# Reciprocal square roots on GpSimd instead of a ten-step VectorE chain

## The chip, the cores and the metric

The kernel runs on one core of one Trainium2 chip. The metric is the device time of one execution in microseconds (us). A profile of one execution shows the core's engines: TensorE (PE; its weight loads are PEld), VectorE (DVE), ScalarE (ACT), GpSimd (POOL), and SyncE (SP), which here issues DMA transfers.

## What is computed

One layer of a hybrid decoder trunk on 1024 tokens of width 1024, in float32: a half feed-forward, a mixer with eight gated-delta heads and sixteen Mamba-2 heads, a second half feed-forward, and a last norm.

```python
def rms_norm(x, w):
    y = x * lax.rsqrt(jnp.mean(x * x, axis=-1, keepdims=True) + EPS)
    return y * w

def l2_normalize(x):
    return x * lax.rsqrt(jnp.sum(x * x, axis=-1, keepdims=True) + EPS)

def reference(x, ...):
    x = x + 0.5 * swiglu(rms_norm(x, ffn1_norm[i]), ffn1_w_gate[i], ffn1_w_up[i], ffn1_w_down[i])
    x = x + hybrid_mixer(rms_norm(x, mix_norm[i]), w_in[i], ...)   # delta heads: l2_normalize of q and k,
                                                                   # rms_norm of each head's output
    x = x + 0.5 * swiglu(rms_norm(x, ffn2_norm[i]), ffn2_w_gate[i], ffn2_w_up[i], ffn2_w_down[i])
    return rms_norm(x, final_norm)
```

Every norm has one reciprocal square root per token (per token and head in the delta heads, per token and group in the Mamba-2 gate norm).

## The kernel before

The tokens lie in eight blocks of 128 (NB = 8), one token per partition, so the reciprocal roots of a block are one column of 128 values. Each big product is made of three passes of TensorE with operands split in a high and a low part (`mm3`, lines 121 to 123; lines 332 to 334 and 552 to 554 are the same three passes in the feed-forwards).

The stages in time: the start (blocks loaded, the first half of the blocks normalised in two pairs by `normalise_pairs`, the second half by `normalise(1, ...)`, transposes on TensorE, splits, first gate and up products); the first feed-forward; at its end `norm_first` (blocks 0 to 3, called while the last products of the down projection run) and `norm_second` (blocks 4 to 7, in two pairs); projections and the Mamba-2 heads (about 700 to 1000 us); the delta heads (about 1000 to 1560 us); the out projection, with `normalise(0, ...)` and `normalise(1, ...)` for the second feed-forward; that feed-forward; and `finish`, block by block, for the last norm.

`rsqrt_into` (line 109) is called at each of these places. It makes a first guess from the bits of the value (line 112) and refines it in three rounds of three VectorE instructions (lines 116 to 118): ten instructions, each reading what the one ahead wrote. The input tile is `ssv` (mean square plus epsilon), the output `rstd`; in the Mamba-2 gate norm they are `sv` and `rg`, in the delta heads `tk` and `rin`, `sso` and `co`. What reads the output differs: at the start lines 207 and 208 (in place, on ScalarE and VectorE), in `normalise` lines 186 and 188, in `norm_second` lines 741 and 742 (output `xn`), in `finish` lines 1456 and 1457 (output `xw`). Scaled blocks then go through TensorE's transposes (`transposed`, line 216, into the PSUM tiles `ps_sc`, two buffers), from which ScalarE and VectorE make the operands (`keepx`, `bh`, `bl`, `hhi`, `hlo`).

The program is written in a tile framework. Its scheduler puts each engine's instructions in an order of its own, from the dependences and its estimates of costs; the hints `tc.issue_after` hold some back. On the chip each engine runs its own list strictly in order and waits at an instruction until its inputs are there. GpSimd's list holds, besides constants and the first small loads, 36 memsets of `pre`, 24 selects of 128x1024 (`md`, `dt`) and some memsets for the heads. `ah` is the high part of a gate or up weight (`wst` when it comes from the staging tile), `as` the gate and up weights' sum, `wd` and `hid` the down projection's operands.

Of the kernel before, what the change touches and what calls it, by code (L numbers as in the profile page):

```python
# [11 lines left out]
F32 = mybir.dt.float32  # L12
F32R = mybir.dt.float32r
I32 = mybir.dt.int32
BF16 = mybir.dt.bfloat16
AF = mybir.ActivationFunctionType
ALU = mybir.AluOpType
# [4 lines left out]
P = 128  # L22
L = 1024
D = 1024
NB = L // P
# [19 lines left out]
def kernel(  # L45
# [7 lines left out]
    V, A, G, T = nc.vector, nc.scalar, nc.gpsimd, nc.tensor  # L53
# [3 lines left out]
    const = ctx.enter_context(tc.tile_pool(name="const", bufs=1))  # L57
# [25 lines left out]
                    pattern=[[1, P]], channel_multiplier=-1)  # L83
    ones = const.tile([P, P], F32, name="ones")
    G.memset(ones, 1.0)
    cols = const.tile([P, 96 + 48 + 12 + 9 + 24], F32, name="cols")
    cw_g = cols[:, 0:96].rearrange("p (t c) -> p t c", t=4)
    cw_s = cols[:, 96:144].rearrange("p (t c) -> p t c", t=4)
# [17 lines left out]
        return last, V.tensor_copy(cols, pc[:, 0:189])  # L106


    def rsqrt_into(pool, y, v, tag):

        n = v.shape[1]
        V.tensor_scalar(out=y.bitcast(I32), in0=v.bitcast(I32), scalar1=-0.5,
                        scalar2=1597463007.0, op0=ALU.mult, op1=ALU.add)
        t = pool.tile([P, n], F32, name="rs_t", tag=tag)
        for _ in range(3):
            V.scalar_tensor_tensor(out=t, in0=y, scalar=-0.5, in1=v, op0=ALU.mult, op1=ALU.mult)
            V.tensor_tensor(out=t, in0=t, in1=y, op=ALU.mult)
            V.scalar_tensor_tensor(out=y, in0=t, scalar=1.5, in1=y, op0=ALU.add, op1=ALU.mult)

    def mm3(o, wh, wl, mh, ml, first, last):  # L120
        T.matmul(o, lhsT=wh, rhs=mh, start=first, stop=False)  # L121
# [39 lines left out]
    def rms_stats(pool, xt, b0, nb, junk):  # L161
        ss = pool.tile([P, nb], F32, name="ss")
        for i in range(nb):
            A.activation(out=junk, in_=xt[b0 + i], func=AF.Square, accum_out=ss[:, i:i + 1])
        v = pool.tile([P, nb], F32, name="ssv")
        V.tensor_scalar(out=v, in0=ss, scalar1=1.0 / D, scalar2=EPS, op0=ALU.mult, op1=ALU.add)
        r = pool.tile([P, nb], F32, name="rstd")
        rsqrt_into(pool, r, v, "rst")
        return r

    def normalise(half, pool, xt, tags=None, jtag=None):
# [20 lines left out]
    def normalise_pairs(pool, xt, jtag):  # L192

        junk = ha.tile([P, 2, D], BF16, name="junk2", tag=jtag)
        sums = [pool.tile([P, 2], F32, name="ss") for _ in range(2)]
        A.activation(out=junk[:, 0], in_=xt[0], func=AF.Square, accum_out=sums[0][:, 0:1])
        V.scalar_tensor_tensor(out=junk[:, 1], in0=xt[1], scalar=1.0, in1=xt[1],
                               op0=ALU.mult, op1=ALU.mult, accum_out=sums[0][:, 1:2])
        for i in range(2):
            sq = A.activation(out=junk[:, 0], in_=xt[2 + i], func=AF.Square, accum_out=sums[1][:, i:i + 1])  # L200
        for i in range(2):
            v = pool.tile([P, 2], F32, name="ssv")
            V.tensor_scalar(out=v, in0=sums[i], scalar1=1.0 / D, scalar2=EPS, op0=ALU.mult, op1=ALU.add)
            r = pool.tile([P, 2], F32, name="rstd")
            rsqrt_into(pool, r, v, "rst")
            with tc.issue_after(sq.ins):
                A.mul(out=xt[2 * i], in_=xt[2 * i], mul=r[:, 0:1])
            last = V.tensor_scalar(out=xt[2 * i + 1], in0=xt[2 * i + 1], scalar1=r[:, 1:2], scalar2=None,
                                   op0=ALU.mult)
        return xt[0:4], last  # L210
# [476 lines left out]
    with ExitStack() as c1:  # L687
        npool = NormPool(ffn_pools(c1))
        H = {}
        with tc.tile_pool(name="x1", bufs=1, side="right", reuse_waits="tile") as xp, \  # L690
                tc.tile_pool(name="keep", bufs=1, side="right", reuse_waits="tile") as kp:
            xt = blocks(xp, "xt")
            for b in range(4):
                nc.sync.dma_start(out=xt[b], in_=x_v[:, b])
            last_t, cols_in = load_cols(npool)
            raws = [a_load(ffn1_w_gate[0], 0), a_load(ffn1_w_up[0], 0)]
            for b in range(4, NB):
                nc.sync.dma_start(out=xt[b], in_=x_v[:, b])
            ops = [{}, {}]
            x0, last = normalise_pairs(npool, xt, "h6")  # L700
            with tc.issue_after(last.ins), tc.issue_after(cols_in.ins):
                a_start(npool, raws, ops, 0)
            r11, r22 = (kp.tile([P, 4, 512], F32, name=f"keepx{i}") for i in range(2))
            with tc.issue_after(last_t.ins):
                b_first(npool, x0, nrm[0], H, r11)
            x1 = normalise(1, npool, xt, jtag="h7")
            a_start(npool, raws, ops, 1)
            last = b_second(npool, x0, x1, nrm[0], H, r11, r22,
                     start_rest(npool, H, ffn1_w_gate[0], ffn1_w_up[0], raws, ops))
        dn = gate_up_phase(0, npool, H, ffn1_w_gate[0], ffn1_w_up[0], ffn1_w_down[0], raws, ops, last)  # L710

        xp = c1.enter_context(tc.tile_pool(name="x1b", bufs=1, side="right", reuse_waits="tile"))
        xt = blocks(xp, "xtb")
        h2 = []

        def norm_first():
            h2.extend(new_ht())
            for b in range(4):
                nc.sync.dma_start(out=x_scr[:, b], in_=xt[b])
            norm_ht(0, normalise(0, npool, xt), nrm[1], *h2)  # L720

        ss = const.tile([P, 8], F32, name="ss2")
        xns = []

        def square(i, dh):
            junk = npool.tile([P, 512], BF16, name="junk", tag="q")
            A.activation(out=junk, in_=xt[4 + i][:, dh * 512:(dh + 1) * 512], func=AF.Square,
                         accum_out=ss[:, 4 * dh + i:4 * dh + i + 1])

        def norm_second(i):  # L730
            square(i, 0)
            nc.sync.dma_start(out=x_scr[:, 4 + i], in_=xt[4 + i])
            if i % 2 == 0:
                return
            v = npool.tile([P, 2], F32, name="ssv")
            V.tensor_tensor(out=v, in0=ss[:, i - 1:i + 1], in1=ss[:, 3 + i:5 + i], op=ALU.add)
            V.tensor_scalar(out=v, in0=v, scalar1=1.0 / D, scalar2=EPS, op0=ALU.mult, op1=ALU.add)
            r = npool.tile([P, 2], F32, name="rstd")
            rsqrt_into(npool, r, v, "rst")
            xn = hbp[0].tile([P, 2, D], F32, name="xn", tag=("b3", "b0")[i // 2])  # L740
            A.mul(out=xn[:, 0], in_=xt[3 + i], mul=r[:, 0:1])
            V.tensor_scalar(out=xn[:, 1], in0=xt[4 + i], scalar1=r[:, 1:2], scalar2=None, op0=ALU.mult)
            xns.extend((xn[:, 0], xn[:, 1]))
            if i == 3:
                h2.append(norm_ht(1, xns, nrm[1], *h2))

        def before_last():
            load_gates_w()
            prefetch()

        with tc.tile_pool(name="dtmp0", bufs=1, reuse_waits="tile") as dtmp:
            down_all(dtmp, xt, x_v, dn, [before_last], norm_first, lambda i: square(i, 1), norm_second)
        hhi, hlo, last_h = h2

    cm = ExitStack()
    gp = cm.enter_context(tc.tile_pool(name="gates", bufs=1, reuse_waits="tile"))
# [53 lines left out]
    with tc.tile_pool(name="gtmp", bufs=1, side="right", reuse_waits="tile") as tp:  # L810
# [48 lines left out]
        for c in (15, 13, 11, 9, 7, 5, 3):  # L859
# [8 lines left out]
                               in1=alog.unsqueeze(1).to_broadcast([P, NB, NG]),  # L868
# [31 lines left out]
    for un in range(4):  # L900
# [138 lines left out]
        if un % 2 == 1:  # L1039
            pc = psum("mx")  # L1040
            for b in range(NB):
                T.matmul(pc[:, 2 * b:2 * b + 2], lhsT=sq[:, b * P:(b + 1) * P], rhs=ones[:, 0:2],
                         start=True, stop=True)
            sv = const.tile([P, NB], F32, name=f"sv{grp}")
            V.tensor_scalar(out=sv, in0=pc[:, 0:2 * NB].rearrange("p (b c) -> p b c", c=2)[:, :, 0],
                            scalar1=1.0 / 512.0, scalar2=EPS, op0=ALU.mult, op1=ALU.add)
            rg = const.tile([P, NB], F32, name=f"rg{grp}")
            rsqrt_into(gp, rg, sv, "rst")
            rstd_g.append(rg)
    cs_.close()  # L1050

# [49 lines left out]
    with ExitStack() as cg:  # L1101
        g1 = cg.enter_context(tc.tile_pool(name="gdn1", bufs=1, reuse_waits="tile"))
        g2 = cg.enter_context(tc.tile_pool(name="gdn2", bufs=2, reuse_waits="tile"))
        for h in range(GH):
# [59 lines left out]
            vr = g2.tile([P, NB, P], F32, name="vr")  # L1164
            ssq = g2.tile([P, NB], F32, name="ssq")
            rin = g2.tile([P, NB], F32, name="rin")
            rsqrt_into(g2, rin, tk, "rst")
            V.tensor_tensor(out=rin, in0=rin, in1=tk, op=ALU.mult)
            for half in range(2):
                pt = psum("mx")  # L1170
# [131 lines left out]
                A.activation(out=jk, in_=vr[:, b], func=AF.Square, accum_out=sso[:, b:b + 1])  # L1302
            V.scalar_tensor_tensor(out=sso, in0=sso, scalar=1.0 / P, in1=cq, op0=ALU.mult, op1=ALU.add)
            co = g2.tile([P, NB], F32, name="co")
            rsqrt_into(g2, co, sso, "rsto")
            V.tensor_tensor(out=vr, in0=vr, in1=co.unsqueeze(2).to_broadcast([P, NB, P]), op=ALU.mult)
            nc.sync.dma_start(out=mix_scr[h // 2][:, :, hl * P:(hl + 1) * P], in_=vr)

# [139 lines left out]
    def finish(i):  # L1448
# [2 lines left out]
        V.scalar_tensor_tensor(out=v, in0=ss[:, i:i + 1], scalar=1.0 / D, in1=ss[:, 4 + i:5 + i],  # L1451
                               op0=ALU.mult, op1=ALU.add)
        r = npool.tile([P, 1], F32, name="rstd")
        rsqrt_into(npool, r, v, "rst")
        o = xw[i // 2][:, i % 2]
        A.mul(out=o[:, 512:], in_=o[:, 512:], mul=r)
        V.tensor_scalar(out=o[:, 0:512], in0=o[:, 0:512], scalar1=r, scalar2=None, op0=ALU.mult)
# [28 lines left out]
```

## Time and profile before

| | |
|---|---|
| time, median of 3 runs | 2310.83 us (2310.03 to 2311.5) |
| span of the profiled execution | 2309.8 us |
| PE busy | 2275.9 us, 99% |
| DVE busy | 1726.7 us, 75%, 3349 instructions |
| ACT busy | 1096.0 us, 47% |
| POOL busy | 53.6 us, 2%, 125 instructions |
| DMA traffic | 281.33 MB, mean 122 GB/s |

Of the profiled execution the span is known, 2309.8 us, and no other time; the median of the runs lies 1.03 us above it. Busy is the time in which an engine had an instruction running. In a row of a timeline the first number is the start in us from the start of the span, the second the duration in us; the brackets at the end give the engine's idle time ahead of it and what ended that.

### The profile page before, as it was taken

The page shows a single profiled execution, that of the slowest core. Times are in us where ns is not written, and L with a number is a line of the kernel's source. Part 1 is how long each engine was busy: PE and PEld are TensorE (multiplying, and loading weights), DVE is VectorE, ACT ScalarE, POOL GpSimd, SP SyncE. Part 2 cuts the span into 40 slices and gives each one's busy share as a digit, 9 for nine tenths or more (in the row PEclk, how much of TensorE's full clock was granted, in tenths as well). Part 3 has the DMA queues.
Part 4 walks back from the last instruction along what each step waited for, and adds up shares of the span by engine and source line. Part 5 has one row for each costly group of instructions (what it writes and reads, how often), then busy time and mean ns, then how long its engine had stood idle before and what let it go on. Part 6 is the DMA issues. An engine that isn't in the chain of part 4 may idle for free.

```text
span 2309.8 us, 31485 instructions
## 1 busy us (share of the span) xinstructions
PE 2275.9 (99%) x11766; PEld 1868.7 (81%) x11766; DVE 1726.7 (75%) x3349; ACT 1096.0 (47%) x1990; POOL 53.6 (2%) x125
## 2 busy tenths in 40 slices
PE   7999999999999999999999999999999999999998
PEld 5788888888878888888888888888878888888886
DVE  7977776767765675668778888778698777766787
ACT  7433333343367785864455556422543333334344
POOL 0000000000000100000000000000000000000000
PEclk9999999999999999999999999999999999999999
DMA  3333332573652322222333222335223333329456
GB/s 111 125 114 103 105 108 98 175 279 129 220 180 78 92 92 74 72 86 74 83 101 82 73 83 61 116 98 192 91 83 116 111 102 105 109 88 349 141 156 214
DMA packets 220957, 281.33 MB, mean 122 GB/s; under 512 B 47008, under 2 KB 153564, under 8 KB 219780
## 3 DMA queue, kind: packets, MB, share of 16 engines
q1 hardware_dynamic: 220548, 279.23, 37.4%
q8 instruction: 92, 1.51, 0.3%
q14 instruction: 61, 0.50, 0.1%
q0 software_dynamic: 256, 0.10, 0.0%
HBM read 211.55 MB, written 67.73 MB: 121 GB/s over the span
## 4 chain that ended last, share of the span: by engine, by line
PE 89%; DVE 5%; ACT 2%; DMA 1%; issue 1%; SPq 0%; POOL 0%; DVEq 0%; ACTq 0%
PE ps_pj L123 11%; PE ps_pj L122 10%; PE ps_pj L121 10%; PE ps_pj L332 6%; PE ps_pj L334 6%; PE ps_pj L333 6%; PE ps_mx L332 3%; PE ps_mx L334 3%; PE ps_mx L333 3%; PE ps_pj L553 2%; PE ps_pj L554 2%; PE ps_pj L552 2%; PE ps_oo L334 2%; PE ps_oo L333 2%; PE ps_oo L332 2%; PE ps_sc L552 1%
## 5 line engine op out<-in xcount | busy, mean ns | idle before, releaser
L123 PE MATMUL ps_pj<-hhi,wlo 128*128 128x512 f32 x832 | 334.3, 402 | 0.0
L121 PE MATMUL ps_pj<-hhi,whi 128*128 128x512 f32 x832 | 332.8, 400 | 0.4 <-ACT gsb L826 0.4
L122 PE MATMUL ps_pj<-hlo,whi 128*128 128x512 f32 x832 | 332.2, 399 | 0.0
L334 PE MATMUL ps_pj<-bh,al 128*128 128x512 f32 x688 | 267.9, 389 | 0.0
L333 PE MATMUL ps_pj<-bl,ah 128*128 128x512 f32 x688 | 267.8, 389 | 0.0
L332 PE MATMUL ps_pj<-bh,ah 128*128 128x512 f32 x688 | 267.5, 390 | 0.0
L121 PEld LDWEIGHTS ps_pj<-hhi,whi 128*128 128x128 f32 x832 | 156.7, 188 | 28.8 <-ACT gsb L826 0.8
L123 PEld LDWEIGHTS ps_pj<-hhi,wlo 128*128 128x128 f32 x832 | 156.7, 188 | 28.5 <-issue 0.7
L122 PEld LDWEIGHTS ps_pj<-hlo,whi 128*128 128x128 f32 x832 | 156.7, 188 | 27.9
L239 ACT CAST ah<-wst 128x512 fp32r<-128x512 f32 x88 | 54.6, 622 | 210.8 <-PE ps_oo L333 125.3
L239 ACT CAST hid<-hraw 128x1024 fp32r<-128x1024 f32 (+1 forms) x84 | 82.3, 981 | 145.5 <-PE ps_oo L554 60.6
L333 PEld LDWEIGHTS ps_pj<-bl,ah 128*128 128x128 f32 x688 | 129.2, 188 | 26.8
L334 PEld LDWEIGHTS ps_pj<-bh,al 128*128 128x128 f32 x688 | 129.1, 188 | 26.6
L332 PEld LDWEIGHTS ps_pj<-bh,ah 128*128 128x128 f32 x688 | 128.9, 188 | 26.6
L315 DVE TENSOR_TENSOR as<-wst 128x512 f32<-128x512 f32 x220 | 145.0, 684 | 2.1 <-DMA wst<-in_ffn_w_up_dram 1.8
L240 DVE TENSOR_TENSOR al<-as,ah 128x512 fp32r<-128x512 f32 x220 | 141.0, 685 | 5.0 <-ACT ah L239 4.5
L332 PE MATMUL ps_mx<-bh,ah 128*128 128x512 f32 x352 | 138.6, 396 | 3.8 <-ACT m L341 1.4
L333 PE MATMUL ps_mx<-bl,ah 128*128 128x512 f32 x352 | 138.2, 393 | 0.4 <-DVE bl L240 0.4
L334 PE MATMUL ps_mx<-bh,al 128*128 128x512 f32 x352 | 137.7, 391 | 0.3 <-DVE al L240 0.3
L239 ACT CAST ah<-as 128x512 fp32r<-128x512 f32 x220 | 125.0, 617 | 20.8 <-DVE as L315 20.8
L240 DVE TENSOR_TENSOR hid<-hraw,hid 128x1024 fp32r<-128x1024 f32 (+1 forms) x84 | 95.0, 1131 | 32.8 <-ACT hid L239 32.5
L341 ACT COPY m<-ps_pj 128x512 f32<-128x512 f32 x88 | 51.5, 588 | 123.1 <-PE ps_pj L334 120.9
(448 smaller groups left out, 5118.9 us busy)
## 6 DMA issues: line engine op xcount, KB each, us to landing
hraw<-hid_scr SPq DMA_DIRECT2D x70, 512.0 KB, 4.4
hid_scr<-hs SPq DMA_DIRECT2D x110, 256.0 KB, 2.3
wst<-in_ffn_w_down_dram SPq DMA_DIRECT2D x50, 512.0 KB, 4.7
wst<-in_ffn_w_gate_dram SPq DMA_DIRECT2D x22, 1024.0 KB, 5.7
wst<-in_ffn_w_up_dram SPq DMA_DIRECT2D x22, 1024.0 KB, 5.4
wst<-in_w_in_dram SPq DMA_DIRECT2D x36, 512.0 KB, 5.2
hid_scr<-sg SPq DMA_DIRECT2D x44, 256.0 KB, 2.0
keep<-in_ffn_w_down_dram SPq DMA_DIRECT2D x20, 512.0 KB, 6.2
```

The lines of the kernel that those rows point to most:

```text
L121: T.matmul(o, lhsT=wh, rhs=mh, start=first, stop=False)
L122: T.matmul(o, lhsT=wh, rhs=ml, start=False, stop=False)
L123: T.matmul(o, lhsT=wl, rhs=mh, start=False, stop=last)
L239: return (A.copy(out=hi, in_=src), V.tensor_tensor(out=lo, in0=src, in1=hi.bitcast(F32), op=ALU.subtract))
L240: V.tensor_tensor(out=lo, in0=src, in1=hi.bitcast(F32), op=ALU.subtract))
L315: V.tensor_tensor(out=t, in0=v[0], in1=v[1], op=v[2])
L332: T.matmul(bank, lhsT=wh[:, k], rhs=bh[:, k], start=a, stop=False, skip_group_check=True)
L333: T.matmul(bank, lhsT=wh[:, k], rhs=bl[:, k], start=False, stop=False, skip_group_check=True)
L334: T.matmul(bank, lhsT=wl[:, k], rhs=bh[:, k], start=False, stop=z, skip_group_check=True)
L341: A.copy(out=t, in_=bank)
L552: T.matmul(bank, lhsT=hh, rhs=wh, start=first and k == 0, stop=False, skip_group_check=True)
L553: T.matmul(bank, lhsT=hh, rhs=wl, start=False, stop=False, skip_group_check=True)
```

## The change

`rsqrt_into` becomes one GpSimd instruction, a power of two tensors: the value and a constant tile `mhalf` of -0.5, filled once at the start by a GpSimd memset. All 31 calls change with it: 310 VectorE instructions go, 31 powers and one memset come, on tiles of 128x1 (4), 128x2 (4), 128x4 (5) and 128x8 (18). The scratch tile `rs_t` goes too.

```diff
+    mhalf = const.tile([P, NB], F32, name="mhalf")
+    G.memset(mhalf, -0.5)
...
-    def rsqrt_into(pool, y, v, tag):
-
-        n = v.shape[1]
-        V.tensor_scalar(out=y.bitcast(I32), in0=v.bitcast(I32), scalar1=-0.5,
-                        scalar2=1597463007.0, op0=ALU.mult, op1=ALU.add)
-        t = pool.tile([P, n], F32, name="rs_t", tag=tag)
-        for _ in range(3):
-            V.scalar_tensor_tensor(out=t, in0=y, scalar=-0.5, in1=v, op0=ALU.mult, op1=ALU.mult)
-            V.tensor_tensor(out=t, in0=t, in1=y, op=ALU.mult)
-            V.scalar_tensor_tensor(out=y, in0=t, scalar=1.5, in1=y, op0=ALU.add, op1=ALU.mult)
+    def rsqrt_into(y, v):
+
+        G.tensor_tensor(out=y, in0=v, in1=mhalf[:, 0:v.shape[1]], op=ALU.pow)
...
-        rsqrt_into(pool, r, v, "rst")
+        rsqrt_into(r, v)
```

The other calls change in the same way. Behind the edit every line number is five lower in the changed kernel (line 207 becomes 202, line 216 becomes 211).

The scheduler orders the engines anew. On ScalarE at the start (`xt` are the blocks, `ah` the high part of the first gate weights, `keepx` the transposed first half), the list before:

```order
L200 ACTIVATE junk_228,ss<-xt 128x1024 x2
L207 ACTIVATE xt<-xt,rstd 128x1024 x2
L239 CAST ah<-wst 128x512
L264 ACTIVATE keepx_281<-ps_sc,cols 128x512
L239 CAST ah<-as 128x512
L239 CAST ah<-wst 128x512
L239 CAST bh_289<-keepx_281 128x512
```

and in the changed kernel:

```order
L195 ACTIVATE junk_230,ss<-xt 128x1024 x2
L234 CAST ah<-wst 128x512
L202 ACTIVATE xt<-xt,rstd 128x1024 x2
L259 ACTIVATE keepx_263<-ps_sc,cols 128x512
L234 CAST ah<-as 128x512
L234 CAST ah<-wst 128x512
L234 CAST ah<-as 128x512
L234 CAST bh_271<-keepx_263 128x512
```

The first cast of the gate weights now stands ahead of the two scalings, and one cast more ahead of `bh`.

On TensorE in `norm_first`, at the first transposes of the scaled blocks (`xtb_3706` to `xtb_3709` before, `xtb_3678` to `xtb_3681` after), the last products of one step of the down projection (four groups of six: three `ps_pj` tiles, then `ps_oo`) stand around them, before:

```order
L554 MATMUL ps_pj_4557<-wd_4943,hid_4944 128x512
L552 MATMUL ps_oo_4558<-wd_4943,hid_4944 128x512
L553 MATMUL ps_oo_4558<-wd_4943,hid_4944 128x512
L216 MATMUL ps_sc_5001<-ident_171,xtb_3706 128x128
L216 MATMUL ps_sc_5008<-ident_171,xtb_3706 128x128
L216 MATMUL ps_sc_5001<-ident_171,xtb_3707 128x128
```

and in the changed kernel:

```order
L549 MATMUL ps_pj_4527<-wd_4915,hid_4916 128x512
L547 MATMUL ps_pj_4528<-wd_4915,hid_4916 128x512
L548 MATMUL ps_pj_4528<-wd_4915,hid_4916 128x512
L211 MATMUL ps_sc_4963<-ident_171,xtb_3678 128x128
L211 MATMUL ps_sc_4963<-ident_171,xtb_3679 128x128
L211 MATMUL ps_sc_4970<-ident_171,xtb_3678 128x128
```

The transposes moved ahead from the second product of the fourth tile (`ps_oo`) to the second product of the second (`ps_pj_4528`): twelve products.

On VectorE at the end (`xt2b` the blocks, `xw` the output; the accumulate into `xt2b` is that of the last block), before:

```order
L116 SCALAR_TENSOR_TENSOR rs_t<-rstd,ssv 128x1
L558 SCALAR_TENSOR_TENSOR xt2b<-ps_oo,xt2b 128x512
L117 TENSOR_TENSOR rs_t<-rs_t,rstd 128x1
L1434 TENSOR_TENSOR xw<-xt2b,wrow 128x512
L118 SCALAR_TENSOR_TENSOR rstd<-rs_t,rstd 128x1
L1451 SCALAR_TENSOR_TENSOR ssv<-ss_18263 128x1
L1457 TENSOR_SCALAR xw<-xw,rstd 128x512
```

and in the changed kernel:

```order
L1446 SCALAR_TENSOR_TENSOR ssv<-ss_18005 128x1
L1452 TENSOR_SCALAR xw<-xw,rstd 128x512
L553 SCALAR_TENSOR_TENSOR xt2b<-ps_oo,xt2b 128x512
L1429 TENSOR_TENSOR xw<-xt2b,wrow 128x512
L1446 SCALAR_TENSOR_TENSOR ssv<-ss_18005 128x1
L1452 TENSOR_SCALAR xw<-xw,rstd 128x512
```

The third block's scaling (line 1457, now 1452), which stood behind the last accumulate, stands ahead of it, and waits there for that block's power on GpSimd.

More of the change, by code (lines that the diff above doesn't have):

```diff
@@ L204, in normalise_pairs @@
             r = pool.tile([P, 2], F32, name="rstd")
-            rsqrt_into(pool, r, v, "rst")
+            rsqrt_into(r, v)
             with tc.issue_after(sq.ins):
@@ L738, in norm_second @@
             r = npool.tile([P, 2], F32, name="rstd")
-            rsqrt_into(npool, r, v, "rst")
+            rsqrt_into(r, v)
             xn = hbp[0].tile([P, 2, D], F32, name="xn", tag=("b3", "b0")[i // 2])
@@ L1047 @@
             rg = const.tile([P, NB], F32, name=f"rg{grp}")
-            rsqrt_into(gp, rg, sv, "rst")
+            rsqrt_into(rg, sv)
             rstd_g.append(rg)
@@ L1166 @@
             rin = g2.tile([P, NB], F32, name="rin")
-            rsqrt_into(g2, rin, tk, "rst")
+            rsqrt_into(rin, tk)
             V.tensor_tensor(out=rin, in0=rin, in1=tk, op=ALU.mult)
@@ L1304 @@
             co = g2.tile([P, NB], F32, name="co")
-            rsqrt_into(g2, co, sso, "rsto")
+            rsqrt_into(co, sso)
             V.tensor_tensor(out=vr, in0=vr, in1=co.unsqueeze(2).to_broadcast([P, NB, P]), op=ALU.mult)
@@ L1453, in finish @@
         r = npool.tile([P, 1], F32, name="rstd")
-        rsqrt_into(npool, r, v, "rst")
+        rsqrt_into(r, v)
         o = xw[i // 2][:, i % 2]
```

## The prediction

> **What bounds the kernel now.** I read the page first: engines, the slices of the span and the head of the chain that ended last.
>
> ```profile
> PE 2275.9 (99%) x11766; PEld 1868.7 (81%) x11766; DVE 1726.7 (75%) x3349; ACT 1096.0 (47%) x1990; POOL 53.6 (2%) x125
> ...
> PE   7999999999999999999999999999999999999998
> ...
> PE 89%; DVE 5%; ACT 2%; DMA 1%; issue 1%; SPq 0%; POOL 0%; DVEq 0%; ACTq 0%
> ```
>
> TensorE is busy in 99% of the span and makes 89% of the chain that set the end. Only the first and the last slice show 7 or 8 tenths. Work taken off VectorE can therefore pay only where TensorE waits, so the next view is TensorE's waits over the whole run, and then a table by stretch (columns: busy time and count of PE, PEld, DVE, ACT, POOL, granted clock, DMA share, GB/s).
>
> ```profile
> PE ps_mx L104 <- DMA colst<-in_gdn_conv_w_dram: 7.4, 1, 7.4
> ...
> PE ps_sc L216 <- ACT xt L207: 2.0, 2, 1.6
> ...
> PE ps_sc L216 <- ACT xtb L186: 1.0, 1, 1.0
> ...
> PE ps_sc L216 <- ACT xt L186: 0.3, 1, 0.3
> ...
> PE ps_sc L216 <- ACT xn L741: 0.3, 1, 0.3
> ...
> 14.50:30.00 15.50, 13.83 (x54) 10.04 (x54) 13.76 (x25) 15.09 (x29) 0.00 (x0) 1.00 0.33 129
> ...
> 1300.00:1500.00 200.00, 198.81 (x1337) 161.99 (x1336) 159.02 (x523) 104.32 (x242) 7.84 (x26) 1.00 0.31 91
> ```
>
> The waits that end in a normalised tile (xt, xtb, xn) are where reciprocal roots stand ahead of TensorE: 2.0 + 1.0 + 0.3 + 0.3 = 3.6 us. The clock column is 1.00, so time lost or won is lost or won in waits. In the middle of the delta-rule heads TensorE is busy 198.81 of 200 us: at most 1.2 us of such a stretch is to be had.
>
> **What goes, and what comes.** One chain, by its first instruction in its four groups, and then all that GpSimd does which could price a power:
>
> ```profile
> L112 DVE TENSOR_SCALAR rstd<-ssv x13: 145/170/171, 7.6 to 2303.7; 128x4 int32<-128x4 int32 x5, 128x2 int32<-128x2 int32 x4, 128x1 int32<-128x1 int32 x4
> L112 DVE TENSOR_SCALAR rin<-tk x8: 149/150/151, 1015.2 to 1456.8; 128x8 int32<-128x8 int32 x8
> L112 DVE TENSOR_SCALAR co<-sso x8: 161/164/171, 1103.3 to 1562.4; 128x8 int32<-128x8 int32 x8
> L112 DVE TENSOR_SCALAR rg<-sv x2: 164/165/166, 847.8 to 985.7; 128x8 int32<-128x8 int32 x2
> ...
> L895 POOL TENSOR_SCALAR_AFFINE_SELECT dt<-dt 128x1024 f32<-128x1024 f32 x8 | 13.5, 1687 | 79.6 <-ACT qe L1126 46.1 <-PE ps_pj L123 33.4
> ...
> L776 POOL MEMSET pre<- 128x3 f32 x36 | 3.7, 102 | 1081.1 <-PE ps_oo L554 661.7 <-DVE qt L784 221.2 <-DVE xs L784 70.4
> ...
> L82 POOL TENSOR_SCALAR_AFFINE_SELECT triu<-triu 128x128 f32<-128x128 f32 x1 | 0.3, 293 | 0.0
> masks.py:199 POOL TENSOR_SCALAR_AFFINE_SELECT ident<-ident 128x128 f32<-128x128 f32 x1 | 0.3, 292 | 0.0
> ```
>
> There are 13 + 8 + 8 + 2 = 31 chains, so 310 VectorE instructions of about 0.16 us, some 50 us of its 1726.7, go. 31 powers of one to eight columns come, and one memset of the exponent (0.10 us by the row of the 128x3 memset, in a stretch where GpSimd only issues loads: nothing).
>
> No row shows a power. Call its duration d. Below, d is at least 0.10 us (the 128x3 memset, which reads nothing); above, I take 1.69 us (the select on 1024 columns). The tiles here have one to eight columns, so the fixed cost counts, and the 0.10 and 0.29 us rows are nearest in size; but a power of two tensors must do more per element than a select. I take d = 0.6 us for all shapes, an estimate, and write every place as a function of d. The Trainium skill ("GPSIMD Engine Reference", section 4.1, engine selection) puts elementwise work on VectorE and calls GpSimd about two times slower with two inputs; by that rule on its own the power would be near twice one 0.16 us row, d = 0.3. No run shows that so far, and the sum by it would be 2309.7.
>
> The scheduler orders every engine anew, and that matters more than the 50 us. It puts the consumers of the reciprocal root ahead by what the chain took. Five places follow.
>
> **Place A, the start.** The second pair of blocks (lines as in the kernel before):
>
> ```profile
> 2.20 7.68 DMA xt<-in_x_dram
> ...
> wst<-in_ffn_w_up_dram SPq DMA_DIRECT2D x1, 1024.0 KB, 12.3
> ...
> 3.46 1.72 SPq L301 DMA_DIRECT2D wst<-in_ffn_w_up_dram  x1
> ...
> 11.14 0.17 DVE L203 TENSOR_SCALAR ssv<-ss 128x2 f32<-128x2 f32 x1 [0.79 <-ACT junk L200]
> ...
> 13.31 1.15 ACT L207 ACTIVATE xt<-xt,rstd 128x1024 f32<-128x1024 f32 x1 [1.16 <-DVE rstd L118]
> ...
> 14.36 0.60 ACT L239 CAST ah<-wst 128x512 fp32r<-128x512 f32 x1
> ...
> 14.51 1.94 PE L216 MATMUL ps_sc<-ident,xt 128*128 128x128 f32 x7 [1.62 <-ACT xt L207]
> ...
> 15.93 1.03 ACT ah L239 x2
> ```
>
> The x loads of the front had landed at 9.88 (2.20 + 7.68), the first up weights land at 15.76 (3.46 + 12.3), and the gate weights lie between the two in the queue; I take the middle, 12.8 us, an estimate. In the kernel before ScalarE scales both blocks (L207) and then casts the gate weights; in the changed one the cast comes first. So ScalarE, in order, waits to 12.8, casts to 13.35, and runs the two L207 to 15.6; TensorE's transposes start at 15.6, not 14.51: 1.1 us later, and d does not enter below about 2 us (the second power has from 11.3 to 13.35). Behind keepx now stand three casts ahead of bh, not two (the chain's row at 15.93: 0.52 us each), so the first product is 1.1 + 0.5 = 1.6 us later. ScalarE is the bound of this stretch (15.09 busy of 15.50), so it does not catch that up. Then comes the second half's normalisation: its chain goes, but TensorE meets those transposes 18 and more products earlier, so what the chain gives is waited away. I take +1.5 us for the whole start, from -1 (the 2.0 us of waits there go, the cast finds its data) to +4 (the transposes also wait for a PSUM buffer behind the four ah casts that now stand ahead on ScalarE).
>
> **Place B, norm_first, at the end of the first feed-forward.**
>
> ```profile
> 639.72 0.17 DVE L166 TENSOR_SCALAR ssv<-ss 128x4 f32<-128x4 f32 x1 [1.33 <-ACT junk L164]
> ...
> 640.11 0.19 ACT L727 ACTIVATION_READ_ACCUMULATOR junk<-xtb 128x1 f32 x1
> ...
> 643.04 2.19 ACT L186 ACTIVATE xtb<-xtb,rstd 128x1024 f32<-128x1024 f32 x2
> ...
> 640.31 0.39 PE L554 MATMUL ps_pj<-wd,hid 128*128 128x512 f32 x1
> ...
> 642.80 0.39 PE L553 MATMUL ps_oo<-wd,hid 128*128 128x512 f32 x1
> ...
> 644.24 0.94 PE L216 MATMUL ps_sc<-ident,xtb 128*128 128x128 f32 x4 [1.05 <-ACT xtb L186]
> ```
>
> Eleven products lie between 640.31 and 642.80, 0.226 us each. Before, TensorE was free for the transposes at 642.80 + 0.23 = 643.03 and began at 644.24: 1.21 us of gap, 1.20 after the start of L186. After, they stand 12 products earlier, at 640.31. L186 starts when ScalarE is free (640.30) or when the power is done (639.89 + 0.05 + 0.03 + d = 639.97 + d), and the gap is 1.20 after that: max(1.19, 0.86 + d). The second scaled block follows 1.1 us behind, as only two products separate the two transposes: 0.2 more. Change: max(1.19, 0.86 + d) + 0.2 - 1.21, at d = 0.6 +0.45. The 1.93 us that the chain frees buy nothing, because the slot moves as well.
>
> **Place C, norm_second, and place D, the second half's normalisation before the second feed-forward.** The row that waits in each:
>
> ```profile
> 672.58 1.15 ACT L741 ACTIVATE xn<-xtb,rstd 128x1024 f32<-128x1024 f32 x1 [1.42 <-DVE rstd L118]
> ...
> 1664.94 2.19 ACT L186 ACTIVATE xt<-xt,rstd 128x1024 f32<-128x1024 f32 x2 [0.84 <-DVE rstd L118]
> ```
>
> A chain that runs alone takes 1.93 us (10 steps, as in the last rows below). In C the two groups of transposes stand five and four products earlier (1.13 and 0.90 us), the chains save 1.93 - d each, and the accumulate of the last block is queued on VectorE behind xn, which now waits for the first power: (1.13 - 1.93 + d) + (0.90 - 1.93 + d) + d = 3d - 1.83, not under -0.3, the wait that the row of TensorE's waits shows. At 0.6 it is 0.0. In D the transposes stand six products earlier, 1.36 us: 1.36 - 1.93 + d = d - 0.57, not under -0.3; at 0.6, 0.0. In D L186 also moves ahead of the copy of m2f on ScalarE; before, ScalarE sat idle 0.84 us ahead of L186, and I take that as the copy's slack, at no cost. normalise(0) there is not waited for by TensorE at all.
>
> **The heads, 700 to 1500 us.** Two rg, eight rin and eight co chains (18 x 1.6 us of VectorE) were hidden behind TensorE's 198.81 of 200; the powers are hidden by the same work. They queue on GpSimd ahead of pre memsets and selects, whose idle time is in the hundreds of us (661.7 on one releaser), so they wait for nobody. Nothing, give or take the 1.2 us of that row. If that cover went, 18 d = 11 us would show.
>
> **Place E, the end.**
>
> ```profile
> 2300.92 0.39 PE L554 MATMUL ps_oo<-wd,hid 128*128 128x512 f32 x1
> ...
> 2301.73 0.69 DVE L558 SCALAR_TENSOR_TENSOR xt2b<-ps_oo,xt2b 128x512 f32<-128x512 f32 x1
> ...
> 2302.45 0.69 DVE L1434 TENSOR_TENSOR xw<-xt2b,wrow 128x512 f32<-128x512 f32 x1
> ...
> 2303.26 0.16 DVE L1451 SCALAR_TENSOR_TENSOR ssv<-ss 128x1 f32<-128x1 f32 x1
> ...
> 2303.73 0.15 DVE L112 TENSOR_SCALAR rstd<-ssv 128x1 int32<-128x1 int32 x1
> ...
> 2305.66 0.49 DVE L1457 TENSOR_SCALAR xw<-xw,rstd 128x512 f32<-128x512 f32 x1
> ```
>
> Before, the last accumulate stands inside the third block's chain, and the last chain runs from 2303.73 to 2305.66, 1.93 us. TensorE ends at 2301.31 (2300.92 + 0.39). After, VectorE has nothing but the third block's scaling ahead, so the accumulate can start at 2301.35 (0.38 earlier), ssv follows at 2302.88, ends at 2303.05, and the scaling starts at 2303.1 + d, not 2305.66: 2.5 - d sooner, 1.9 at d = 0.6. The transfers behind move with it. From d = 1.3 on, the three earlier powers, each waited for in order by a scaling on VectorE, hold the last accumulate back, and each further us costs three.
>
> **Sum.** Start +1.5, B +0.45, C 0.0, D 0.0, heads 0, end -1.9: +0.05 us at d = 0.6. At d = 0.10: +1.5 +0.2 -0.3 -0.3 -2.4 = -1.3. At d = 1.69: +1.5 +1.55 +3.24 +1.1 and at the end -0.8 + 1.2 = +0.4, in all +7.8. The profiled span of 2309.8 us becomes 2309.9; the median of the three runs, 2310.83, lies 1.0 us above that span, so I take 2311.0 us.
>
> **Rivals.**
> 1. The power is dear. Every place is a power in series with TensorE's queue, and the sum climbs by 7.1 us for each us of d between 0.6 and 1.69. At 1.69 the time is 2318.6. Slower by over 0.2%, 4.6 us, from d = 1.25 on (0.2% is about what a measurement of this kernel can tell from no change). For it: a power is more than a select, and two tensors are read. Against it: eight columns at most, where 128 columns of a select cost 0.29. 0.25.
> 2. The waits fall away. Places A to D lose their 3.6 us of waits without new ones, and the end wins 2.4: 2304.8. It needs d near 0.10 and the cast at place A to find its weights before 11 us. For it: 2.0 us of waits end in L207. Against it: the moved slots in B and D, which the code's new order fixes. 0.13.
> 3. The first power pays once for something that later ones don't. The first reciprocal root starts at 7.6 us (first group of the chain rows) and is needed by L207 only after the gate's cast, at 13.4: 5.8 us are free, and each us beyond delays the start by one, the second power queued behind adding d. A first use of 6.5 us gives 0.7 + 0.6, or 2312.3. Against it: the first select on GpSimd took 292 ns and the second 293. 0.10, and within 0.2% either way. The Trainium skill ("GPSIMD Engine Reference", section 2.1, instruction dispatch) has the first call to a freshly loaded kernel pay about 6 us without an instruction in the profile; by that figure alone an estimate of the loss is 0.2 + 0.6 us, still inside 0.2%. No run here shows such a load so far.
>
> **How the numbers follow.** Forecast with its unknown d between 0.1 and 1.25: 0.52; with rival 3, within 0.2%: 0.62. Slower 0.25, faster 0.13. The range leaves half of rival 2 and a third of rival 1 out: from 2307.0 to 2319.0. The forecast's own range is 2309.5 to 2315.4.
>
> **What would show it.** In the profile after: GpSimd rows of a power with their mean (0.6 expected, B to E follow from it); VectorE's count down by 310; the first L207 behind the cast of the gate weights at about 13.4 and TensorE's transposes at 15.6; a wait of 1.2 to 1.7 on xtb at norm_first with the transposes 12 products earlier; the last scaling's start 2.5 - d nearer to TensorE's end than it was. I am wrong if d is over 1.25, if the gate weights land at another time than 12.8 (the start then moves one for one), or if the heads show TensorE waiting for rin or co.

## The result and the profile after

The changed kernel takes 2325.66 us (median of five runs, 2322.72 to 2330.09) against 2310.47 us of the kernel before (also five runs): a ratio of 1.0064, 95% interval 1.0054 to 1.0075. It is 15.2 us slower, where 2311.0 us was forecast, and outside the range. The profiled execution (2329.4 us) has a span of 2327.6 us, 17.8 us above the 2309.8 before.

The page after: engines, TensorE's and the clock's slices, and the chain's head.

```profile
PE 2283.8 (98%) x11766; PEld 1875.2 (81%) x11766; DVE 1692.3 (73%) x3039; ACT 1094.1 (47%) x1990; POOL 95.3 (4%) x157
...
PEclk9999999999999999998999999999999999999999
...
PE 77%; DVE 10%; issue 5%; ACT 3%; DMA 3%; POOL 1%; SPq 1%; POOLq 0%; DVEq 0%; ACTq 0%
```

VectorE lost its 310 instructions, but TensorE's share of the chain fell from 89% to 77% and VectorE's rose from 5% to 10%. One slice of the clock shows an 8. The powers, grouped by shape (busy, mean ns of one, GpSimd's idle time ahead):

```profile
L113 POOL TENSOR_TENSOR co<-sso,mhalf 128x8 f32<-128x8 f32 x8 | 13.1, 1640 | 126.2 <-DVE sso L1298 126.2
L113 POOL TENSOR_TENSOR rin<-tk,mhalf 128x8 f32<-128x8 f32 x8 | 13.1, 1639 | 101.0 <-DVE tk L1143 101.0
...
L113 POOL TENSOR_TENSOR rstd<-ssv,mhalf 128x4 f32<-128x4 f32 x5 | 6.6, 1323 | 1348.7 <-DVE ssv L161 1348.7
L113 POOL TENSOR_TENSOR rg<-sv,mhalf 128x8 f32<-128x8 f32 x2 | 5.2, 2582 | 16.4 <-DVE sv L1040 16.4
...
L113 POOL TENSOR_TENSOR rstd<-ssv,mhalf 128x2 f32<-128x2 f32 x4 | 3.2, 812 | 35.8 <-DVE ssv L732 31.3 <-DVE ssv L198 4.5
...
L113 POOL TENSOR_TENSOR rstd<-ssv,mhalf 128x1 f32<-128x1 f32 x4 | 2.5, 625 | 24.9 <-DVE ssv L1446 24.9
```

The mean duration grows with the columns, 0.63 us for one and 1.64 for eight (rin and co); 0.6 for all shapes holds for one column alone. Where it goes, by VectorE's waits and then TensorE's between 1000 and 1595 us (the heads):

```profile
DVE vr L1301 <- POOL co L113: 12.3, 8, 1.8
...
DVE rin L1163 <- POOL rin L113: 11.2, 8, 1.6
...
PE ps_sc L1269 <- DVE sn L1288: 2.2, 3, 0.8
PE ps_sc L1220 <- DVE lv L1214: 1.7, 2, 1.4
```

VectorE stands still for 23.5 us in sixteen waits, nearly as long as the sixteen chains had kept it busy (16 x 1.6 us). So VectorE won next to nothing in the heads. TensorE's waits listed there come to 9.0 us in eight rows, two of which stand above (lv and sn are tiles of the delta heads). Before, they came to 1.3 us, in two rows:

```profile
PE ps_pj L121 <- DVE xa L1343: 0.8, 2, 0.7
PE ps_sc L1246 <- ACT lv L1239: 0.5, 3, 0.2
```

The first such place in the second head, VectorE and then TensorE:

```profile
1069.60 0.17 DVE L1144 RECIPROCAL br<-tk 128x2 f32<-128x2 f32 x1
1071.38 0.17 DVE L1163 TENSOR_TENSOR rin<-rin,tk 128x8 f32<-128x8 f32 x1 [1.62 <-POOL rin L113]
1071.46 0.15 DVE L1145 TENSOR_TENSOR br<-br,beta 128x2 f32<-128x2 f32 x1
1071.56 0.45 DVE L1214 STREAM_TRANSPOSE lv<-lv 128x256 f32<-128x256 f32 x1
...
1072.06 0.21 PE L1220 MATMUL ps_sc<-lv,u 32*32 32x32 f32 x1 [1.41 <-DVE lv L1214]
```

The multiplication behind the power (L1163) waits 1.62 us, and the transposition of lv, which needs nothing of rin, is queued behind it. TensorE waits 1.41 us for lv. In the kernel before the same place reads:

```profile
1064.67 0.15 DVE L112 TENSOR_SCALAR rin<-tk 128x8 int32<-128x8 int32 x1
1064.79 0.16 DVE L1150 TENSOR_TENSOR br<-br,beta 128x2 f32<-128x2 f32 x1
1064.97 0.45 DVE L1219 STREAM_TRANSPOSE lv<-lv 128x256 f32<-128x256 f32 x1
...
1067.56 0.16 DVE L117 TENSOR_TENSOR rs_t<-rs_t,rin 128x8 f32<-128x8 f32 x1
```

There the chain had begun, but lv went between two of its steps, and the rest of the chain ran in time that nobody waited for. Ten short steps can be spread; one wait can't.

What follows the 1.41 us is dearer than the wait. The table by stretch (PE, PEld, DVE, ACT, POOL busy and count, then the granted clock), at the start and behind 1072 us:

```profile
28.00:33.00 5.00, 2.37 (x9) 1.30 (x10) 3.40 (x7) 2.81 (x5) 2.59 (x1) 0.97 0.01 2
33.00:38.00 5.00, 3.60 (x15) 2.92 (x14) 3.82 (x6) 4.75 (x10) 0.00 (x0) 0.50 0.00 0
38.00:43.00 5.00, 5.00 (x28) 4.23 (x27) 3.78 (x6) 3.90 (x9) 0.00 (x0) 0.84 0.01 3
...
1074.00:1077.00 3.00, 3.00 (x53) 1.96 (x54) 0.54 (x2) 0.91 (x5) 0.00 (x0) 0.50 0.66 173
1077.00:1087.00 10.00, 10.00 (x56) 8.82 (x57) 3.87 (x7) 2.33 (x10) 0.00 (x0) 0.50 0.22 63
```

The clock falls to 0.50 at both places. Each stretch's shortfall from 1.00, doubled, is its time at half clock: 0.3 + 5.0 + 1.6 = 6.9 us at the start, and 13 us and a little more in the head. Half of it is lost where TensorE has work throughout: up to 3.5 + 6.5 = 10 us of the 17.8. The rest, near 8 us, is left for waits; that is about what TensorE's waits in the heads grew by (9.0 against 1.3). The Trainium skill ("TensorE: Matmul & The Clock Gate", Part 1) has the clock drop to 4/8 after an idle window of about 3.4 us and return after a busy one. The half clock and the lengths (6.9 is twice 3.4, 13 to 14 four times) agree. That TensorE must be idle for a whole 3.4 us does not, since the gap here is 1.4 us, and 1.9 at the start, with gaps of 0.7 and 0.5 us shortly ahead of it. That a busy window brings the clock back does not either: TensorE is busy for all 13 us of the last two rows, at 0.50. Nor is a gap of 1.4 us always followed by a fall: in the profile of the run with powers for rin alone (below) TensorE waits 1.43 us for lv at this very place, and the clock stays at 1.00. What decides is not shown. Such periods come and go between executions: the five runs of this kernel spread over 7 us, from 2322.72 us at a granted clock of 0.998 to 2330.09 at 0.994.

### The profile page after: what moved, and what is told of

It is laid out like the page before. It is cut to its first block, busy times and chain, and to the rows that moved or that the text cites. A ratio compares the mean times of both kernels' runs of the same rounds, so it can differ in the third digit from the quotient of the medians.

```text
span 2327.6 us, 31217 instructions
## 1 busy us (share of the span) xinstructions
PE 2283.8 (98%) x11766; PEld 1875.2 (81%) x11766; DVE 1692.3 (73%) x3039; ACT 1094.1 (47%) x1990; POOL 95.3 (4%) x157
## 4 chain that ended last, share of the span: by engine, by line
PE 77%; DVE 10%; issue 5%; ACT 3%; DMA 3%; POOL 1%; SPq 1%; POOLq 0%; DVEq 0%; ACTq 0%
PE ps_pj L116 7%; PE ps_pj L118 7%; PE ps_pj L117 7%; PE ps_pj L327 6%; PE ps_pj L328 6%; PE ps_pj L329 6%; PE ps_mx L327 3%; PE ps_mx L328 3%; PE ps_mx L329 3%; PE ps_pj L548 2%; PE ps_pj L549 2%; PE ps_pj L547 2%; PE ps_oo L328 2%; PE ps_oo L329 2%; PE ps_oo L327 2%
```

## The experiments

Theory W says that the power's duration counts where an engine waits for it in order, and for what is queued behind, with the clock's fall on top. All times are medians of 5 or 11 runs, each against the kernel before on the same chip, whose median moved from 2310.25 to 2311.53 us between the four groups of runs, on three chips. In the edits `power_into` is the one GpSimd instruction and `rsqrt_into` the chain.

**A short operation in the same order.**

```diff
-        G.tensor_tensor(out=y, in0=v, in1=mhalf[:, 0:v.shape[1]], op=ALU.pow)     # mhalf = -0.5
+        G.tensor_tensor(out=y, in0=v, in1=mhalf[:, 0:v.shape[1]], op=ALU.mult)    # mhalf = 0.03
```

> Every one of the 31 powers is a multiplication by the constant 0.03 on GpSimd instead, on the same tiles and in the very order of the changed kernel on each engine; the norms are therefore not computed. Theory W (waiting: the power's duration, 0.54 to 1.64 us alone, stands in series in VectorE's and ScalarE's queues): the multiplication lasts 0.1 to 0.4 us, VectorE's waits for rin and co fall from 23.5 us to under 6, and the time is 2308 to 2313 us, no half clock in the heads. Rival O (the new order alone loses, whatever the duration): 2318 to 2326 us, as the changed kernel. Rival P (VectorE and GpSimd disturb each other): nearer to 2320.

2310.38 us, -1.15 (ratio 0.9996, 0.9987 to 1.0005); this kernel leaves out the norms, since no root is computed. The multiplication of 128x8 takes 0.20 us, the wait at the same instruction is 0.18, not 1.62, and VectorE's waits for rin and co come to 1.6 us, not 23.5:

```profile
L123 POOL TENSOR_TENSOR rin<-tk,mhalf 128x8 f32<-128x8 f32 x8 | 1.6, 202 | 108.7 <-DVE tk L1153 108.7
...
1066.43 0.17 DVE L1173 TENSOR_TENSOR rin<-rin,tk 128x8 f32<-128x8 f32 x1 [0.18 <-POOL rin L123]
```

With the very order of the changed kernel on every engine the loss is gone. So the order loses nothing for itself (rival O falls); it loses because it puts the readers where only a short operation is done in time.

**The chain in the heads, and powers in the heads alone.** Of the calls, 18 (rin, co, rg) go back to the chain, or these 18 alone become powers:

```diff
-            power_into(rin, tk)
+            rsqrt_into(g2, rin, tk, "rst")     # and co, rg; the other kernel has it the other way round
```

> The chain again for rin, co and rg (18 calls in the heads), powers at the other 13 places. Theory W: what is left is the start (+3 us, of it 3.4 by 6.8 us at half clock), norm_first and norm_second (+1.3), the end (-1.9): 2312 to 2315 us, VectorE does not wait for GpSimd between 1000 and 1575 us. Rival S (the start and the clock carry the loss): 2320 or more.

> Powers for rin, co and rg alone, the chain at the other 13 places. Theory W: the waits of VectorE in the heads (23.5 us in 16 waits) cost TensorE 5 to 8 us, and 3.4 us more in each execution in which its clock falls to half there: 2316 to 2322 us. Rival S: 2310 to 2313 us.

The chain in the heads: 2315.00 us, +3.5 (1.0017, 1.0008 to 1.0026), at the upper end of the range expected. Powers in the heads alone: 2323.26 us, +11.7 (1.0048, 1.0036 to 1.0061), 1.3 above the range; VectorE's 12.3 and 11.2 us of waits are there again, to the tenth. The two sum to 15.2, the whole loss. Rival S falls: three quarters of it lie in the heads.

**rin and co, each alone.**

> Powers for rin alone (eight of 128x8), the chain at the other 23 places. Theory W: VectorE waits 11 us for rin at the multiplication that makes rin ready, and the transposition of lv, from which TensorE's next small products come, is queued behind it: 2315 to 2319 us, TensorE waits for lv. Rival C (it is co that costs, since the serial substitution ft, fx stands behind it): 2310 to 2312 us.

> Powers for co alone (eight of 128x8), the chain at the other 23 places. Theory W: VectorE waits 12 us for co at the scaling of vr, and the substitution queued behind it is late by as much: 2313 to 2318 us; with rin alone the two losses make up that of both (11.7 us). Rival R (only rin costs): 2310 to 2312 us.

rin alone: 2322.65 us, +12.4 (1.0053, 1.0039 to 1.0066), from 2317.89 at a granted clock of 0.999 to 2325.86 at 0.995: the waits cost some 8 us (2317.9 against 2310), the half clock up to 8 more. That is more than expected. co alone: 2316.85 us, +6.6 (1.0033, 1.0020 to 1.0045). Both rivals fall. The two don't add up as expected (19.0 against 11.7 together, which was measured on another chip): both delay the same substitution and lv, and the clock's part varies between executions; which of these it is was not separated.

**The same powers, read later.** For rin the exponent becomes +0.5, which gives the product directly; for co the scaling is held behind lv of the next head.

```diff
-            power_into(rin, tk)
-            V.tensor_tensor(out=rin, in0=rin, in1=tk, op=ALU.mult)
+            G.tensor_tensor(out=rin, in0=tk, in1=phalf, op=ALU.pow)     # phalf = 0.5
```

```diff
-            V.tensor_tensor(out=vr, in0=vr, in1=co.unsqueeze(2).to_broadcast([P, NB, P]), op=ALU.mult)
-            nc.sync.dma_start(out=mix_scr[h // 2][:, :, hl * P:(hl + 1) * P], in_=vr)
+            late.append(scale_out)             # the same two lines, called in the next head:
...
+            with tc.issue_after(lv_t.ins):     # lv_t: the transposition of lv
+                late.pop()()
```

> As with powers for rin alone, but the exponent is +0.5, so that the power gives rin directly and VectorE's multiplication behind it goes; VectorE first meets rin at the scaling of vr from PSUM, after lv. GpSimd's power lasts 1.64 us as before. Theory W: VectorE waits under 2 us for rin in all, and the time is 2309 to 2312 us. Rival P (GpSimd's power itself disturbs VectorE or the queue of GpSimd): 2315 to 2319 us, as with powers for rin alone.

> As with powers for co alone, but the scaling of vr by co is held back behind the transposition of lv of the next head, so that nothing urgent is queued behind the wait; the last head's stays. Theory W: VectorE waits under 2 us for co, and the time is 2309 to 2312 us. Rival P: as with powers for co alone; rival L (the later write of mix_scr is missed by the out projection): over 2312 us with TensorE waiting there.

rin: 2313.83 us, +3.6 (1.0014, 1.0006 to 1.0023), over the range expected, but 8.8 below the early read; no wait of VectorE for rin is left in the list. What the 3.6 is stays open. TensorE's list in the heads still has 1.4 us for jd and 1.4 for xa, two other tiles there; and in the profiled execution the clock is at half for 3.4 us near 847 and for 3.4 us near 1700 us, away from rin, up to 3.4 us lost together, where the profile of before has 1.00. The last experiment has the same power for rin and no loss. co: 2312.07 us, +1.8 (1.0006, 0.9997 to 1.0015), 4.8 below, just over its range, and not clear of no change. One wait of 1.8 us is left, the last head's, and TensorE's waits in the out projection are those of before, so rival L falls:

```profile
DVE vr L1317 <- POOL co L123: 1.8, 1, 1.8
```

The powers still last 1.65 us, on the same engine and beside the same work, so rival P (the power disturbs by itself) falls for most of the loss.

**The other places.** Powers in the two pairs at the start, in the second half's normalisation at the start, and in the four norms of the middle, each alone:

> Powers in the two pairs of the first half at the start (two of 128x2), the chain at the other 29 places. TensorE's order is that of the kernel before, ScalarE's has the cast of the gate weights ahead of the two scalings. The prediction's place A: the first product 1.6 us later, whatever the power lasts: 2311.5 to 2312.5 us. Rival: later waits at the start (the bound there is ScalarE) take it up: 2310.0 to 2310.8 us.

> A power for the second half's normalisation at the start alone (one of 128x4). Theory W: it is stretched by VectorE's two-input instructions to about 2.6 us, TensorE meets the transposes early, waits 2 us and more, and runs 6.8 us at half clock behind that wait (3.4 us lost): 2311 to 2314 us, a period at half clock near 33 us in most executions. Rival: the wait costs as it did in the prediction, nothing net, and the clock stays full: 2309.5 to 2311 us.

> Powers in norm_first, norm_second and the two normalisations ahead of the second feed-forward (three of 128x4, two of 128x2), the chain elsewhere. By the prediction's formulas with the measured durations (1.01 us for 128x4, 0.70 for 128x2): +0.86 + 0.27 + 0.44 = 1.6 us: 2311.5 to 2312.5 us. Rival: the scheduler's slots cost nothing, 2310 to 2311 us.

The pairs: 2312.73 us, +1.4 (1.0005, 0.9996 to 1.0014), near the number of the prediction's place A, though the interval reaches to no change. The profile does not bear the agreement out. TensorE, in the order of before, is 1.1 us late until norm_first (the product that began at 642.80 begins at 643.93), but the transposes there, which had waited 1.0 us for xtb, no longer wait and begin at 644.28, against 644.24 before:

```profile
643.93 0.39 PE L558 MATMUL ps_oo<-wd,hid 128*128 128x512 f32 x1
644.28 0.94 PE L221 MATMUL ps_sc<-ident,xtb 128*128 128x128 f32 x4
...
846.00:852.00 6.00, 6.00 (x25) 4.93 (x25) 5.47 (x10) 4.75 (x7) 0.09 (x1) 0.72 0.01 3
```

The statistics behind xtb stand where they stood (ssv at 639.76, 639.72 before), so this gap takes the delay up. What the execution is behind at its end it lost near 847 us, where the clock is 0.72 over 6 us: 3.4 us at half clock, 1.7 lost, in a stretch without a power. So that place A costs time at the end is not shown.

The second half: 2313.05 us, +1.7 (1.0010, 1.0001 to 1.0019). Its one power took 2.55 us, and in the profiled execution the clock fell behind it near 33 us for 6.8 us, as expected. The middle: 2314.12 us, +2.8 (1.0015, 1.0006 to 1.0023), above the 1.6 expected. With the next experiment's end, 1.4 + 1.7 + 2.8 - 0.8 + 11.7 = 16.8, near to the 15.2 of all; each term is uncertain by about 2 us.

**The end alone.**

> Powers in finish alone (the last four, 128x1); TensorE's order is that of the kernel before. The prediction's place E: the end comes 2.5 - d = 1.9 us sooner at the measured d = 0.54 to 0.6: 2308.0 to 2309.2 us. Rival: the transfers of the output end it, and nothing is won: 2310.5 us.

2310.77 us, -0.8 (0.9996, 0.9987 to 1.0005): short of the 1.9 expected, and nothing that can be told from no change. In the profile the 1.9 us are there and something else has taken them:

```profile
2302.44 0.39 PE L559 MATMUL ps_oo<-wd,hid 128*128 128x512 f32 x1
...
2305.23 0.49 DVE L1462 TENSOR_SCALAR xw<-xw,rstd 128x512 f32<-128x512 f32 x1 [0.66 <-POOL rstd L123]
```

From TensorE's end (2302.44 + 0.39) to the last scaling are 2.40 us, against 4.35 before; but TensorE ended 1.5 us later than in the profile of before, with the same order. A table by stretch of the same execution shows the clock at 0.72 over 6 us near 1700 us, 3.4 us at half clock and 1.7 us lost, where the profile of before has 1.00. Nine of the fourteen profiled executions, this one and that of the pairs among them, have such a period near 847 or 1700 us, and that of before has none; as long as these come and go, two microseconds can't be told.

```profile
1697.00:1703.00 6.00, 5.51 (x17) 4.43 (x18) 5.85 (x10) 2.69 (x5) 0.00 (x0) 0.72 0.61 195
```

**The places without an urgent wait, together.** rin by the power of +0.5, co read late, and finish.

> The places that theory W leaves without an urgent wait, together: rin by a power of +0.5, co by a power with its scaling held back behind lv of the next head, and finish; the chain at the other eleven places. Theory W: VectorE waits under 6 us for GpSimd in all, and the time lies within 3 us of the kernel before, 2309 to 2313 us, against 2323 with the same powers in the heads read at once. Rival P (the power on GpSimd disturbs by itself): 2317 us or more.

2310.65 us against 2310.64 (0.9998, 0.9989 to 1.0007; 2307.00 to 2313.09). VectorE's waits for GpSimd come to 3.6 us, under the 6 expected. Twenty powers cost nothing that can be measured here, and bring nothing; rival P falls. No version tried is faster than the kernel before by more than the measurement tells.

## Why the prediction was wrong, point by point

**The duration.** d = 0.6 for all shapes was the first error. Alone on its engine the power takes 0.54 us (128x1), 0.70 (128x2), 1.01 (128x4) and 1.64 (128x8). Beside VectorE instructions with two SBUF inputs it stretches: the first row is undisturbed, and the last overlaps three of them, which themselves take 0.68 to 0.69 us, as elsewhere. The second overlaps a scaling of 128x1024 on VectorE, which reads one such tile.

```profile
7.40 0.72 POOL L113 TENSOR_TENSOR rstd<-ssv,mhalf 128x2 f32<-128x2 f32 x1 [1.28 <-DVE ssv L198]
11.35 1.13 POOL L113 TENSOR_TENSOR rstd<-ssv,mhalf 128x2 f32<-128x2 f32 x1 [3.23 <-DVE ssv L198]
28.27 2.59 POOL L113 TENSOR_TENSOR rstd<-ssv,mhalf 128x4 f32<-128x4 f32 x1 [15.79 <-DVE ssv L161]
```

The selects of before (0.29 us for 128 columns) were no guide, since a power costs some 0.16 us for each column: (1.64 - 0.54) / 7. The stretched ones, up to 2.6 us, lie beyond the 1.69 that the prediction took as its upper bound. By the rule of two times VectorE (the Trainium skill, "GPSIMD Engine Reference", section 4.1, as the prediction drew on it) it would be 0.3; the multiplication at 0.20 us is near to that, the power is not. Rival 3 falls by the first row: the first power starts 0.15 us behind the end of its input ssv (7.25) and takes no longer than others of its shape.

**The heads, 0 us: the term that failed.** "The powers are hidden by the same work" looked at TensorE's and GpSimd's idle time, and at who waits for GpSimd's other work. It did not ask what is queued on VectorE behind the instruction that waits for the power, though the changed kernel's order has it: the multiplication (line 1163) ahead of lv (line 1214). In place of 0 the 18 powers of the heads cost 11.7 us on their own, by waits and by the clock's fall. The sign that was named, TensorE waiting for rin or co, did not come in that form: VectorE waits for them, and TensorE for lv and sn. The number named for the case that the cover goes, 18 d = 11 us, is by chance near the 11.7 measured; the mechanism is the wait, not the cover of GpSimd.

**The clock.** "The clock column is 1.00, so time lost or won is lost or won in waits" held for the profile of the kernel before, not for that of the changed kernel, where a wait of 1.4 us was followed by 13 us at half clock.

**Place A, +1.5.** Right up to the first product: the cast of the gate weights waits, and to nearly the time forecast (12.8, an estimate).

```profile
12.90 0.62 ACT L234 CAST ah<-wst 128x512 fp32r<-128x512 f32 x1 [1.83 <-DMA wst<-in_ffn_w_gate_dram]
13.42 2.18 ACT L202 ACTIVATE xt<-xt,rstd 128x1024 f32<-128x1024 f32 x2
16.39 0.69 ACT L259 ACTIVATE keepx<-ps_sc,cols 128x512 f32<-128x512 f32 x1 [0.78 <-PE ps_sc L211]
...
19.19 1.22 PE L327 MATMUL ps_mx<-bh,ah 128*128 128x512 f32 x2 [0.95 <-ACT bh L234]
```

Before, keepx and the first product stood here:

```profile
15.24 0.69 ACT L264 ACTIVATE keepx<-ps_sc,cols 128x512 f32<-128x512 f32 x1 [0.27 <-PE ps_sc L216]
...
17.52 1.31 PE L332 MATMUL ps_mx<-bh,ah 128*128 128x512 f32 x2 [0.43 <-ACT bh L239]
```

The first product comes 1.67 us later; 1.6 was said, and its two parts are there: keepx is 1.15 us later, and one more cast of 0.52 stands ahead of bh. TensorE's first transposes start at 14.62, not 15.6, since the first block is ready by then. But a late first product is not a late end: in the profile of the pairs alone norm_first takes the delay up, which the prediction did not ask. The second half's normalisation was taken as even, and cost 1.7 us on its own, with a stretched power and the clock's fall.

**Places B, C and D.** TensorE's waits for normalised tiles there, after:

```profile
PE ps_sc L211 <- ACT xn L736: 1.8, 2, 0.9
...
PE ps_sc L211 <- ACT xtb L181: 0.9, 1, 0.9
...
PE ps_sc L211 <- ACT xt L181: 0.9, 1, 0.9
```

At B the wait on xtb is 0.9 us where 1.0 stood before; the formula gave +0.86 at the measured d, but with the slot 0.37 us behind the power's start (640.31 against 639.94). After, it lies 1.14 us behind: TensorE is free at 643.76 + 0.23 = 643.99, the power starts at 642.85.

```profile
643.76 0.39 PE L548 MATMUL ps_pj<-wd,hid 128*128 128x512 f32 x1
...
642.85 1.01 POOL L113 TENSOR_TENSOR rstd<-ssv,mhalf 128x4 f32<-128x4 f32 x1 [611.99 <-DVE ssv L161]
```

Against the forecast TensorE comes to the slot 3.7 us later, and the statistics only 2.9 us, so the wait shrinks by the difference. At C the waits rise from 0.3 to 1.8; the formula gave +0.3, and why it is more stays open. At D the wait rises from 0.3 to 0.9, where the formula gave +0.44. The four norms of the middle alone cost 2.8 us where their formulas gave 1.6.

**Place E, -1.9.** Right: from TensorE's end at 2320.99 the last scaling starts 2.39 us later, at 2323.38, against 4.35 before: 1.96, and the formula 2.5 - d with d = 0.54 gives 1.96.

```profile
2320.60 0.39 PE L549 MATMUL ps_oo<-wd,hid 128*128 128x512 f32 x1
...
2323.38 0.49 DVE L1452 TENSOR_SCALAR xw<-xw,rstd 128x512 f32<-128x512 f32 x1 [0.66 <-POOL rstd L113]
```

**Rival 1** named a dear power with 4.6 us from d = 1.25 on. Its direction was right, but its price came from places B to E, and the loss lies in the heads.

## What to carry to other kernels

When a chain of short instructions on a busy engine is replaced by one on an idle engine, the busy engine saves nothing if it then waits in order for the result: look at what is queued behind the first reader, and move that reader, or remove it, before moving the work. A scheduler that orders a slow instruction as it orders a short one (here the power and the multiplication got the same order) puts the reader early, and that turns the duration into a stall; compare the same order with a short operation to tell the two apart. Count a new wait of TensorE with the half clock that can follow it, and follow a delay to the next place where TensorE waited anyway.

## What the runs showed of the hardware

- A float power of two tensors on GpSimd takes 0.54 us for 128x1 and about 0.16 us for each column more; a multiplication of 128x8 takes 0.20 us.
- VectorE instructions with two SBUF inputs stretch a power on GpSimd: the same 128x4 power takes 1.01 us alone and 2.59 beside three of them, which take their usual 0.68 to 0.69, and a 128x8 one 2.58 instead of 1.64 (rg). The Trainium skill ("GPSIMD Engine Reference", section 1, specifications) names VectorE instructions with two SBUF inputs as a source of contention for the shared interfaces; these rows agree.
- TensorE's granted clock fell to 0.50 behind a gap of 1.4 us in a stretch that is otherwise dense, for 13 us, and behind one of 1.9 us at the start, for 6.9; behind the same gap of 1.4 us in another kernel's profile it did not fall.
